# A hybrid decoder step on one core: prompt attention with float32r sums over keys, two heads in turn, and 16 page buffers

## The chip, the core and the metric

One NeuronCore of a Trainium2 chip runs the whole program. The engines work side by side, each through its own queue in order: PE (TensorE, matrix products; PEld is its loading of weights), DVE (VectorE), ACT (ScalarE), POOL (GpSimd) and SP (SyncE, which issues most DMAs here). The metric is the device time of one execution in microseconds (us), the median of three runs.

## What is computed

One inference step of a trunk of four layers. Layer 2 is the one with attention; the others mix tokens by a state space model (0, 3) or pooling (1). Each is followed by a feed-forward part (FFN) with a short convolution. There is a prompt of 272 tokens (16 learned ones and 256) and 8 decode sequences of 4 new tokens with 1024 past ones each, whose keys and values lie in 64 pages of 128 tokens in a paged cache. Attention is of the stick-breaking kind, cut to what matters:

```python
z = einsum('bqhd,bshd->bhqs', q, k) * scale + bias          # 16 heads of 64
mask = k_pos[None, :] < q_pos[:, None]
log_not = where(mask, log_sigmoid(-z), 0)
between = cumsum(log_not, axis=3, reverse=True) - log_not   # a sum over later keys
wts = where(mask, exp(log_sigmoid(z) + between), 0)
o = einsum('bhqs,bshd->bqhd', wts, v)
```

So each head needs scores, a softplus of them, a sum of it over all later keys, an exponential, and a weighted sum of values.

## The kernel before

**Precision.** The large projections split each operand in a rounded high half and the rest, both float32r, and add three products (`mm3`, L248 to L250). The attention's own products are float32: the profile shows each of them as two records of PE.

**Weights.** A plan lists all weight blocks and cache pages in order of use. Each goes by DMA from SP's queue into one of 8 places of `raw` (4 KB per partition each); for the pages of attention there are `NX` more places in `rawx`. A planner (`build_plan`) gives each load the place that it reckons to be free first. `split_blocks` makes `hi` (ACT, L208) and `lo` (DVE, L211) of a weight block, four buffers each; pages are used as they come. SP works strictly in the order of the plan, so a load whose place is not free holds back all later ones.

**The attention stage.** After the projection to q, k and v, one loop over units `u` does the decode part: `keys_t(u)` transposes a quarter of four key pages on PE (eight transposes, L1332) and copies them out as `kt` (ACT L1337, DVE L1338); two units later `keys(u)` multiplies them with the queries (four products of 256 columns, L1351, each for one range of 32 columns of the array); `scores`, `weights` and `weights_t` turn 16 units of scores into weights; `values(u)`, six slots of four units behind, multiplies two value pages with them (four products of 512 columns, L1415, in four such ranges). 64 key pages and 64 value pages of 512 KB pass through.

The prompt part is strewn in between from `u` = 22 on, one step every two units, for pairs of heads `d` = 0 to 7: `prompt_z(d)` makes scores z of two heads (L1477, 272 columns for the first 128 keys, L1478, 144 for the next 128), adds bias and mask (L1480) and takes the softplus L (DVE L1268, ACT L1269 and L1270, DVE L1271). `prompt_c(d)` sums L over later keys: a product with a triangle of ones `tri` within a block of 128 keys, one with all `ones` for the block behind it, and one for the last 16 keys (`L2`). z minus that sum (L1496), exponential (L1497). `prompt_o(d)` multiplies the weights with the values of the prompt, head after head (L1506 to L1508); the two heads of a pair write different halves of the columns of one PSUM bank. The order on each engine is set by a scheduler at build time, which starts from this program order.

`kt` has six buffers of 512 columns, two a unit; `wT`, the transposed weights of the decode part, two of 1024 columns.

Of the kernel before, what the change touches and what calls it, by code (L numbers as in the profile page):

```python
# [9 lines left out]
F32 = mybir.dt.float32  # L10
# [6 lines left out]
DM = 1024  # L17
# [23 lines left out]

LAG = 6
LEAD = 2
NX = 5


def bc(ap, pos, n):
# [13 lines left out]
class Trunk:  # L61
# [1211 lines left out]
    def attention(self, l):  # L1273
        nc, I, O = self.nc, self.I, self.O
        v = nc.vector
        with self.tc.tile_pool(name="att", bufs=1) as ap:
# [5 lines left out]
            vp2, vs = vx[64:80], vx[0:32]  # L1282
            self.rawx = ap.tile([128, NX, 1024], F32, name="rawx")
            kp = [ap.tile([128, DM], F32, name="kp", tag="z", bufs=2) for _ in range(2)]
            kp2 = ap.tile([48, DM], F32, name="kp2", tag="wT", bufs=2)

            msk = ap.tile([128, 416], F32, name="msk")
            nc.gpsimd.memset(msk, 0.0)
# [3 lines left out]
                                        fill=NEG, base=-1, channel_multiplier=-1)  # L1292
            tri = ap.tile([128, 128], F32, name="tri")
            nc.gpsimd.affine_select(out=tri, in_=self.ones, pattern=[[-1, 128]], compare_op=ALU.is_ge, fill=0.0, base=0, channel_multiplier=1)
            bB = ap.tile([128, 16], F32, name="bB")
            nc.scalar.dma_start(bB, I["attn_logit_bias"][0].partition_broadcast(128))
            self.build_dec_masks(ap, bB)
# [20 lines left out]
            def keys_t(u):  # L1318

                sl, dd = divmod(u, 4)  # L1320
                key = [self.page("k", sl, i) for i in range(4)]
                if dd == 0:
                    kt["raw"] = [self.key_page(k) for k in key]
                raw = kt["raw"]
                pts = []
                for s in range(2):
                    pt = self.bank()
                    pts.append(pt.rearrange("p (a k) -> p a k", a=2))
                    for r in range(2):
                        d = 4 * r + dd  # L1330
                        for g in range(2):
                            nc.tensor.transpose(pt[:, r * 256 + g * 128:r * 256 + (g + 1) * 128], raw[2 * s + g][:, d * 128:(d + 1) * 128], self.ident)  # L1332
                if dd == 3:
                    for k in key:
                        self.key_done(k)
                kt[u] = [ap.tile([128, 2, 256], F32, name="kt", tag="kt", bufs=6) for _ in range(2)]
                nc.scalar.activation(kt[u][0], pts[0], AF.Copy)  # L1337
                v.tensor_copy(kt[u][1], pts[1])  # L1338

# [38 lines left out]
            def weights_t(p):  # L1378

                w = zw.pop(p)  # L1380
                wT = ap.tile([128, 8, 128], F32, name="wT", tag="wT", bufs=2)
                wn = ap.tile([32, 128], F32, name="wn", tag="wn", bufs=2)
                for i in range(2):
                    pt = self.bank()
# [85 lines left out]
            def prompt_z(d):  # L1470

                PW[d] = []
                for h in range(2):
                    hs = slice(h * 64, h * 64 + 64)
                    head = 2 * d + h
                    pt = self.bank()
                    nc.tensor.matmul(pt[:, 0:NP], kT[hs, d, 0:128], qT[hs, d, 0:NP], start=True, stop=True)  # L1477
                    nc.tensor.matmul(pt[:, NP:416], kT[hs, d, 128:256], qT[hs, d, 128:NP], start=True, stop=True)  # L1478
                    z = ap.tile([128, 416], F32, name="zp", tag="zp", bufs=4)
                    v.scalar_tensor_tensor(z, pt[:, :416], bB[:, head:head + 1], msk, ALU.add, ALU.add)  # L1480
# [3 lines left out]
                    PW[d].append((z, L))  # L1484

            def prompt_c(d):
                for h in range(2):
                    head = 2 * d + h
                    z, L = PW[d][h]
# [226 lines left out]
```

## Time and profile before

| | us |
|---|---|
| median of three runs | 1666.96 |
| the three runs | 1663.04, 1667.83, 1666.96 |
| the profiled execution, device time | 1663.34 |
| its span, first to last instruction | 1661.6 |

| engine | busy us | share of the span |
|---|---|---|
| PE | 1510.3 | 91% |
| PEld | 1391.7 | 84% |
| DVE | 1206.0 | 73% |
| ACT | 829.3 | 50% |
| POOL | 546.8 | 33% |

The profile is one execution on the chip. Its page shows the time that each engine is busy, the span in 40 slices, the DMA queues, the chain of work that ended last (here 61% on PE) and the costliest groups of instructions. The trace behind it can be asked for stretches, for the instructions in order of time, and for who waited for whom. Matmuls are pipelined: records of neighbours overlap, and a product's own duration is longer than the time until the next begins.

### The profile page before, as it was taken

The page shows a single profiled execution, that of the slowest core. Times are in us where ns is not written, and L with a number is a line of the kernel's source. Part 1 is how long each engine was busy: PE and PEld are TensorE (multiplying, and loading weights), DVE is VectorE, ACT ScalarE, POOL GpSimd, SP SyncE. Part 2 cuts the span into 40 slices and gives each one's busy share as a digit, 9 for nine tenths or more (in the row PEclk, how much of TensorE's full clock was granted, in tenths as well). Part 3 has the DMA queues.
Part 4 walks back from the last instruction along what each step waited for, and adds up shares of the span by engine and source line. Part 5 has one row for each costly group of instructions (what it writes and reads, how often), then busy time and mean ns, then how long its engine had stood idle before and what let it go on. Part 6 is the DMA issues. An engine that isn't in the chain of part 4 may idle for free.

```text
span 1661.6 us, 31539 instructions
## 1 busy us (share of the span) xinstructions
PE 1510.3 (91%) x11336; PEld 1391.7 (84%) x11336; DVE 1206.0 (73%) x2513; ACT 829.3 (50%) x1483; POOL 546.8 (33%) x986
## 2 busy tenths in 40 slices
PE   3487999999899999999999988999978578999997
PEld 3376999999789999998665538999978478999997
DVE  6977589985689985644554545989877895699953
ACT  5453466654366563434444434665535333666643
POOL 7945045532265541101000000555283342144400
PEclk9978999999999999999999998999989698999999
DMA  6113455565325554564887796455524113455551
GB/s 114 15 46 120 145 153 160 153 188 164 102 90 163 161 160 150 164 216 142 300 304 273 281 372 175 148 163 158 167 83 127 32 34 94 140 168 171 156 169 47
DMA packets 220960, 256.24 MB, mean 154 GB/s; under 512 B 59045, under 2 KB 171861, under 8 KB 220720
## 3 DMA queue, kind: packets, MB, share of 16 engines
q1 hardware_dynamic: 218292, 249.15, 48.3%
q0 software_dynamic: 2368, 5.08, 0.9%
q8 instruction: 89, 1.46, 0.4%
q14 instruction: 67, 0.55, 0.1%
q10 hardware_dynamic: 144, 0.01, 0.0%
HBM read 246.78 MB, written 6.43 MB: 152 GB/s over the span
## 4 chain that ended last, share of the span: by engine, by line
PE 61%; DVE 8%; POOL 2%; issue 1%; DMA 1%; ACT 1%; SPq 0%; DVEq 0%; POOLq 0%; ACTq 0%
PE bk L248 16%; PE bk L250 16%; PE bk L249 16%; PE bk L1332 4%; PE zs L1351 2%; PE av L1415 2%; DVE lo L211 1%; DVE t L1102 1%; DVE E L1111 1%; PE bk L1491 1%; PE bk L1506 1%; DMA raw<-in_attn_w_o 1%; DVE t L1101 1%; DVE s L648 0%; PE bk L1494 0%
## 5 line engine op out<-in xcount | busy, mean ns | idle before, releaser
L208 ACT ACTIVATE hi<-raw 128x1024 fp32r<-128x1024 f32 x328 | 344.0, 1056 | 283.8 <-PE bk L249 234.7
L248 PE MATMUL bk<-uhi,hi 128*128 128x304 f32 (+1 forms) x1600 | 478.1, 303 | 7.6 <-ACT uhi L374 7.6
L249 PE MATMUL bk<-ulo,hi 128*128 128x304 f32 (+1 forms) x1600 | 482.7, 302 | 1.8 <-DVE ulo L375 1.8
L250 PE MATMUL bk<-uhi,lo 128*128 128x304 f32 (+1 forms) x1600 | 483.1, 303 | 0.0
L211 DVE TENSOR_TENSOR lo<-raw,hi 128x1024 fp32r<-128x1024 f32 x304 | 374.5, 1237 | 140.3 <-ACT hi L208 138.9
L248 PEld LDWEIGHTS bk<-uhi,hi 128*128 128x128 f32 x1600 | 300.1, 189 | 9.4 <-ACT uhi L374 8.8
L249 PEld LDWEIGHTS bk<-ulo,hi 128*128 128x128 f32 x1600 | 302.4, 189 | 3.7 <-DVE ulo L375 3.2
L250 PEld LDWEIGHTS bk<-uhi,lo 128*128 128x128 f32 x1600 | 301.8, 189 | 1.2 <-issue 0.6
L248 PE MATMUL bk<-ghi,hi 128*128 128x304 f32 (+1 forms) x704 | 212.7, 302 | 3.9 <-DVE so L531 3.2
L249 PE MATMUL bk<-glo,hi 128*128 128x304 f32 (+1 forms) x704 | 212.0, 301 | 0.0
L250 PE MATMUL bk<-ghi,lo 128*128 128x304 f32 (+1 forms) x704 | 210.8, 301 | 0.0
L467 ACT ACTIVATE c<-hx,cpT 128x320 f32<-128x320 f32 (+1 forms) x176 | 113.0, 645 | 94.0 <-DVE hx L461 92.8
L211 POOL TENSOR_TENSOR lo<-raw,hi 128x1024 fp32r<-128x1024 f32 x24 | 58.0, 2415 | 291.5 <-ACT hi L208 247.5
L459 POOL COPY hx<-stT 128x16 f32<-128x16 f32 x176 | 91.0, 522 | 159.1 <-DVE c L469 155.0
L248 PEld LDWEIGHTS bk<-ghi,hi 128*128 128x128 f32 x704 | 132.6, 188 | 5.4 <-DVE so L531 4.3
L249 PEld LDWEIGHTS bk<-glo,hi 128*128 128x128 f32 x704 | 132.7, 188 | 0.1
L250 PEld LDWEIGHTS bk<-ghi,lo 128*128 128x128 f32 x704 | 132.4, 189 | 0.0
L464 POOL COPY hp<-hx 128x2 f32<-128x2 f32 x176 | 94.6, 537 | 105.2 <-DVE hx L460 98.5
L460 DVE TENSOR_TENSOR hx<-bk,rstd 128x272 f32<-128x272 f32 (+1 forms) x176 | 76.1, 433 | 31.2 <-PE bk L250 26.1
L469 DVE SCALAR_TENSOR_TENSOR c<-hx,cpT,c 128x320 f32<-128x320 f32 (+1 forms) x176 | 94.8, 540 | 1.1
L468 DVE SCALAR_TENSOR_TENSOR c<-hx,cpT,c 128x320 f32<-128x320 f32 (+1 forms) x176 | 94.6, 540 | 0.8 <-ACT c L467 0.7
L249 PE MATMUL bk<-zlo,hi 128*128 128x304 f32 (+1 forms) x256 | 77.6, 306 | 3.6 <-DVE zlo L1167 3.6
(488 smaller groups left out, 2698.8 us busy)
## 6 DMA issues: line engine op xcount, KB each, us to landing
raw<-in_ffn_w_up SPq DMA_DIRECT2D x352, 256.0 KB
raw<-in_ffn_w_down SPq DMA_DIRECT2D x88, 512.0 KB
raw<-in_cache_v SPq DMA_DIRECT2D x46, 512.0 KB
raw<-in_cache_k SPq DMA_DIRECT2D x34, 512.0 KB
raw<-in_ssm_w_glu SPq DMA_DIRECT2D x64, 256.0 KB
rawx<-in_cache_k SPq DMA_DIRECT2D x30, 512.0 KB
raw<-in_attn_w_qkv SPq DMA_DIRECT2D x24, 512.0 KB
rawx<-in_cache_v SPq DMA_DIRECT2D x18, 512.0 KB
```

Of the source, the lines that this page charges most:

```text
L208: nc.scalar.activation(hi, raw, AF.Copy)
L211: eng.tensor_tensor(lo, raw, hi.bitcast(F32), ALU.subtract)
L248: mm(out, whi, ahi, start=start, stop=False)
L249: mm(out, whi, alo, start=False, stop=False)
L250: mm(out, wlo, ahi, start=False, stop=stop)
L459: nc.gpsimd.tensor_copy(hv[:, :, 0:2], stT[:, ft].rearrange("p (b t) -> p b t", t=2))
L460: nc.vector.tensor_tensor(h[:, 2 + t0:2 + NP], ps[:, t0:NP], self.rstd[:, t0:NP], ALU.mult)
L464: nc.gpsimd.tensor_copy(hp[:, ft], h[:, NP:NP + 2])
L467: nc.scalar.activation(o, h[:, 2 + t1:], AF.Identity, bias=par(3, ft), scale=par(2, ft))
L468: nc.vector.scalar_tensor_tensor(o, h[:, 1 + t1:HEXT - 1], par(1, ft), o, ALU.mult, ALU.add)
L469: nc.vector.scalar_tensor_tensor(o, h[:, t1:HEXT - 2], par(0, ft), o, ALU.mult, ALU.add)
L1332: nc.tensor.transpose(pt[:, r * 256 + g * 128:r * 256 + (g + 1) * 128], raw[2 * s + g][:, d * 128:(d + 1) * 128], self.ident)
```

## The change

In `prompt_z` both heads' products with 272 columns are issued first, then those with 144. The softplus L is split in two float32r halves, `lh` (a rounding copy on ACT) and `ll` (what it leaves, on DVE). In `prompt_c` the five float32 products of a head become two over all 416 columns with a float32r triangle `trr`, two of 144 columns with float32r ones `onr`, and one float32 product for the last 16 keys, which covers both places in one instruction of 2x16 columns. In `prompt_o` the heads take turns. `kt` takes the four `hi` buffers, one a unit, and `wT` the `lo` buffers of the weights, which are idle in this stage; `rawx` has 8 places instead of 5. `kp2` lies with `L`.

```diff
-NX = 5
+NX = 8
...
-            kp2 = ap.tile([48, DM], F32, name="kp2", tag="wT", bufs=2)
+            kp2 = ap.tile([48, DM], F32, name="kp2", tag="L")
...
+            trr, onr = (ap.tile([128, 128], F32R, name=n) for n in ("trr", "onr"))
+            nc.scalar.activation(trr, tri, AF.Copy)
+            nc.scalar.activation(onr, self.ones, AF.Copy)
...
-                kt[u] = [ap.tile([128, 2, 256], F32, name="kt", tag="kt", bufs=6) for _ in range(2)]
+                kt[u] = self.wp.tile([128, 1024], F32, name="kt", tag="hi", bufs=4).rearrange("p (s a k) -> p s a k", s=2, a=2)
+                kt[u] = [kt[u][:, s] for s in range(2)]
...
-                wT = ap.tile([128, 8, 128], F32, name="wT", tag="wT", bufs=2)
+                wT = self.wp.tile([128, 1024], F32, name="wT", tag="lo", bufs=4).rearrange("p (g r) -> p g r", g=8)
...
+                pts = [self.bank() for _ in range(2)]
+                for o, n, ks in ((0, NP, 0), (NP, 144, 128)):
+                    for h in range(2):
+                        hs = slice(h * 64, h * 64 + 64)
+                        nc.tensor.matmul(pts[h][:, o:o + n], kT[hs, d, ks:ks + 128], qT[hs, d, ks:NP], start=True, stop=True)
                 for h in range(2):
-                    hs = slice(h * 64, h * 64 + 64)
...
-                    nc.tensor.matmul(pt[:, 0:NP], kT[hs, d, 0:128], qT[hs, d, 0:NP], start=True, stop=True)
-                    nc.tensor.matmul(pt[:, NP:416], kT[hs, d, 128:256], qT[hs, d, 128:NP], start=True, stop=True)
...
+                    lh = ap.tile([128, 416], F32R, name="Lh", tag="Lh", bufs=2)
+                    ll = ap.tile([128, 416], F32R, name="Ll", tag="Ll", bufs=2)
+                    nc.scalar.activation(lh, L, AF.Copy)
+                    v.tensor_tensor(ll, L, lh.bitcast(F32), ALU.subtract)
+                    PW[d].append((z, lh, ll))
...
-                    nc.tensor.matmul(pc[:, 0:NP], tri, L[:, 0:NP], start=True, stop=False)
-                    nc.tensor.matmul(pc[:, 128:NP], self.ones, L[:, NP:416], start=False, stop=False)
-                    nc.tensor.matmul(pc[:, 256:NP], self.ones[64:80], L2[:, head], start=False, stop=True)
-                    nc.tensor.matmul(pc[:, NP:416], tri, L[:, NP:416], start=True, stop=False)
-                    nc.tensor.matmul(pc[:, 400:416], self.ones[64:80], L2[:, head], start=False, stop=True)
+                    nc.tensor.matmul(pc[:, 0:416], trr, lh, start=True, stop=False)
+                    nc.tensor.matmul(pc[:, 0:416], trr, ll, start=False, stop=False)
+                    nc.tensor.matmul(pc[:, 128:NP], onr, lh[:, NP:416], start=False, stop=False)
+                    nc.tensor.matmul(pc[:, 128:NP], onr, ll[:, NP:416], start=False, stop=False)
+                    nc.tensor.matmul(pc[:, 128:416].rearrange("p (a q) -> p a q", a=2)[:, :, 128:144], self.ones[64:80], bc(L2[:, head], 1, 2), start=False, stop=True)
...
-                for h in range(2):
-                    hs = slice(h * 64, h * 64 + 64)
-                    head = 2 * d + h
-                    es = slice(head * 64, head * 64 + 64)
-                    nc.tensor.matmul(po[hs, 0:NP], vp[:, 0, es], ws[h][:, 0:NP], start=True, stop=False)
-                    nc.tensor.matmul(po[hs, 128:NP], vp[:, 1, es], ws[h][:, NP:416], start=False, stop=False)
-                    nc.tensor.matmul(po[hs, 256:NP], vp2[:, es], w2[:, head], start=False, stop=True)
+                for st in range(3):
+                    for h in range(2):
...
+                        if st == 0:
+                            nc.tensor.matmul(po[hs, 0:NP], vp[:, 0, es], ws[h][:, 0:NP], start=True, stop=False)
+                        elif st == 1:
+                            nc.tensor.matmul(po[hs, 128:NP], vp[:, 1, es], ws[h][:, NP:416], start=False, stop=False)
+                        else:
+                            nc.tensor.matmul(po[hs, 256:NP], vp2[:, es], w2[:, head], start=False, stop=True)
```

The order that the scheduler makes differs on PE, ACT, DVE and SP within this stage, and in a few neighbouring rows after it. First PE at the first sums over keys (`prompt_c(0)`). The rows of before: the transposes of one unit, then one head's sums.

```order
L1332 MATMUL bk<-ident,raw 128x128 x4
L1332 MATMUL bk<-ident,rawx 128x128 x4
L1491 MATMUL bk<-Lp,tri 128x272
L1492 MATMUL bk<-Lp,ones 128x144
L1493 MATMUL bk<-L_8019,ones 128x16
L1494 MATMUL bk<-Lp,tri 128x144
L1495 MATMUL bk<-L_8019,ones 128x16
```

The same place of PE in the changed kernel (`Lh` and `Ll` are the halves `lh` and `ll`, `L_8023` is L2):

```order
L1336 MATMUL bk<-ident,raw 128x128 x8
L1502 MATMUL bk<-Lh,trr 128x416
L1503 MATMUL bk<-Ll,trr 128x416
L1504 MATMUL bk<-Lh,onr 128x144
L1505 MATMUL bk<-Ll,onr 128x144
L1506 MATMUL bk<-L_8023,ones 128x2x16
```

The first sums stay behind the same unit; each head has five products before and after, with other columns.

Next PE at the first outputs (`prompt_o(0)`), with buffer numbers, since the two heads differ by them only (zp_8929 is one head's weights, zp_8939 the other's). Before:

```order
L1415 MATMUL av_9895<-raw_70,wT_9782 32x512 x4
L1506 MATMUL bk_10048<-zp_8929,vp_7936 64x272
L1507 MATMUL bk_10048<-zp_8929,vp_7936 64x144
L1508 MATMUL bk_10048<-z2_8018,vx_7937 64x16
L1506 MATMUL bk_10048<-zp_8939,vp_7936 64x272
L1507 MATMUL bk_10048<-zp_8939,vp_7936 64x144
L1508 MATMUL bk_10048<-z2_8018,vx_7937 64x16
L1332 MATMUL bk_10057<-ident_71,rawx_7938 128x128
```

The same place in the changed kernel:

```order
L1420 MATMUL av_9910<-rawx_7938,wT_9800 32x512 x4
L1519 MATMUL bk_10069<-zp_8966,vp_7936 64x272
L1519 MATMUL bk_10069<-zp_8977,vp_7936 64x272
L1521 MATMUL bk_10069<-zp_8966,vp_7936 64x144
L1521 MATMUL bk_10069<-zp_8977,vp_7936 64x144
L1523 MATMUL bk_10069<-z2_8022,vx_7937 64x16 x2
L1336 MATMUL bk_10078<-ident_71,raw_70 128x128 x4
```

The heads now alternate product by product.

Last PE ahead of the second outputs (`prompt_o(1)`), where the four value products of one call of `values` stand together before:

```order
L1351 MATMUL zs<-kt,qb_8014 32x256 x4
L1415 MATMUL av<-raw,wT 32x512 x2
L1415 MATMUL av<-rawx,wT 32x512 x2
L1506 MATMUL bk<-zp,vp 64x272
L1507 MATMUL bk<-zp,vp 64x144
```

In the changed kernel key products stand between two and two of them:

```order
L1336 MATMUL bk<-ident,raw 128x128 x4
L1420 MATMUL av<-raw,wT 32x512 x2
L1356 MATMUL zs<-kt,qb_8018 32x256 x4
L1420 MATMUL av<-rawx,wT 32x512 x2
L1519 MATMUL bk<-zp,vp 64x272 x2
```

Over the whole stage the value products of before stand in 40 runs of at most four, those of the changed kernel in 42; the key products in 69 and 72.

## Rows read from the trace of the kernel before

**Rows 1.** Stretches: us, engines busy (instructions), clock, DMA share, GB/s.

```profile
785.00:970.00 185.00, 185.00 (x1632) 111.60 (x1630) 97.02 (x171) 82.07 (x158) 2.38 (x10) 1.00 0.82 292
970.00:991.00 21.00, 19.19 (x129) 7.14 (x129) 7.92 (x16) 5.25 (x15) 0.00 (x0) 1.00 1.02 405
```

**Rows 2.** Waits of SP's queue from 771 to 992: total us, times, longest.

```profile
SPq L186 <- PE bk L1332: 83.8, 24, 16.9
```

**Rows 3.** Timeline of PE at the end: start, us, engine, line, operation.

```profile
987.12 1.05 PE L1415 MATMUL av<-rawx,wT 128*32 128x512 f32 x4 [0.23 <-DMA rawx<-in_cache_v]
...
990.99 1.05 PE L1415 MATMUL av<-raw,wT 128*32 128x512 f32 x4 [0.26 <-DMA raw<-in_cache_v]
992.80 0.66 PE L1428 MATMUL bk<-ident,am 128*128 128x128 f32 x4 [0.76 <-ACT am L1421]
999.26 1.38 PE L248 MATMUL bk<-ohi,hi 128*128 128x304 f32 x4 [5.81 <-ACT ohi L1443]
```

**Rows 4.** Timeline of PE, sums of the first two heads.

```profile
821.08 0.62 PE L1491 MATMUL bk<-Lp,tri 128*128 128x272 f32 x2
...
821.88 0.39 PE L1493 MATMUL bk<-L,ones 16*128 16x16 f32 x2
822.20 0.51 PE L1494 MATMUL bk<-Lp,tri 128*128 128x144 f32 x2
...
824.95 0.66 PE L1332 MATMUL bk<-ident,raw 128*128 128x128 f32 x4
```

**Rows 5.** Timeline of PE, float32r products of the projections and their border.

```profile
405.71 0.28 PE L250 MATMUL bk<-shi,pwl 128*128 128x120 f32 x1
405.82 0.27 PE L248 MATMUL bk<-shi,pwh 128*128 128x120 f32 x1
...
767.25 0.30 PE L249 MATMUL bk<-ulo,hi 128*128 128x304 f32 x1
767.39 0.30 PE L250 MATMUL bk<-uhi,lo 128*128 128x304 f32 x1
767.62 0.74 PE L1477 MATMUL bk<-qT,kT 64*128 64x272 f32 x4
```

**Rows 6.** Timeline of PE, outputs of the first two heads.

```profile
835.37 0.67 PE L1506 MATMUL bk<-zp,vp 128*64 128x272 f32 x2
...
836.43 0.67 PE L1506 MATMUL bk<-zp,vp 128*64 128x272 f32 x2
...
837.49 0.33 PE L1332 MATMUL bk<-ident,rawx 128*128 128x128 f32 x1
```

**Rows 7.** Timeline of PE, decode products beside others; scores of two heads.

```profile
848.12 0.64 PE L1351 MATMUL zs<-kt,qb 128*32 128x256 f32 x8
848.57 1.04 PE L1415 MATMUL av<-raw,wT 128*32 128x512 f32 x8
849.54 0.74 PE L1477 MATMUL bk<-qT,kT 64*128 64x272 f32 x4
850.11 0.42 PE L1478 MATMUL bk<-qT,kT 64*128 64x144 f32 x4
850.46 0.33 PE L1332 MATMUL bk<-ident,rawx 128*128 128x128 f32 x1
...
875.79 1.04 PE L1415 MATMUL av<-raw,wT 128*32 128x512 f32 x2
876.76 0.66 PE L1332 MATMUL bk<-ident,rawx 128*128 128x128 f32 x4
```

**Rows 8.** Timelines of ACT, DVE and PE, from scores to sums.

```profile
854.46 0.55 ACT L1270 ACTIVATE Lp<-Lp 128x416 f32<-128x416 f32 x1
855.04 0.59 DVE L1271 TENSOR_TENSOR Lp<-Lp,zp 128x416 f32<-128x416 f32 x1 [0.32 <-ACT Lp L1270]
860.71 0.62 PE L1491 MATMUL bk<-Lp,tri 128*128 128x272 f32 x2
```

More of the change, by code (lines that the diff above doesn't have):

```diff
@@ L1472, in prompt_z @@
                 PW[d] = []
+                pts = [self.bank() for _ in range(2)]
[3 more added lines that the diff above has]
+                        nc.tensor.matmul(pts[h][:, o:o + n], kT[hs, d, ks:ks + 128], qT[hs, d, ks:NP], start=True, stop=True)
                 for h in range(2):
-                    hs = slice(h * 64, h * 64 + 64)
                     head = 2 * d + h
-                    pt = self.bank()
-                    nc.tensor.matmul(pt[:, 0:NP], kT[hs, d, 0:128], qT[hs, d, 0:NP], start=True, stop=True)
-                    nc.tensor.matmul(pt[:, NP:416], kT[hs, d, 128:256], qT[hs, d, 128:NP], start=True, stop=True)
                     z = ap.tile([128, 416], F32, name="zp", tag="zp", bufs=4)
-                    v.scalar_tensor_tensor(z, pt[:, :416], bB[:, head:head + 1], msk, ALU.add, ALU.add)
+                    v.scalar_tensor_tensor(z, pts[h][:, :416], bB[:, head:head + 1], msk, ALU.add, ALU.add)
                     L = ap.tile([128, 416], F32, name="Lp", tag="Lp", bufs=2)
@@ L1483, in prompt_z @@
                         self.softplus(L, z, v)
-                    PW[d].append((z, L))
+                    lh = ap.tile([128, 416], F32R, name="Lh", tag="Lh", bufs=2)
[3 more added lines that the diff above has]
+                    PW[d].append((z, lh, ll))
             def prompt_c(d):
@@ L1488, in prompt_c @@
                     head = 2 * d + h
-                    z, L = PW[d][h]
+                    z, lh, ll = PW[d][h]
                     pc = self.bank()
-                    nc.tensor.matmul(pc[:, 0:NP], tri, L[:, 0:NP], start=True, stop=False)
-                    nc.tensor.matmul(pc[:, 128:NP], self.ones, L[:, NP:416], start=False, stop=False)
-                    nc.tensor.matmul(pc[:, 256:NP], self.ones[64:80], L2[:, head], start=False, stop=True)
-                    nc.tensor.matmul(pc[:, NP:416], tri, L[:, NP:416], start=True, stop=False)
-                    nc.tensor.matmul(pc[:, 400:416], self.ones[64:80], L2[:, head], start=False, stop=True)
+                    nc.tensor.matmul(pc[:, 0:416], trr, lh, start=True, stop=False)
[3 more added lines that the diff above has]
+                    nc.tensor.matmul(pc[:, 128:416].rearrange("p (a q) -> p a q", a=2)[:, :, 128:144], self.ones[64:80], bc(L2[:, head], 1, 2), start=False, stop=True)
                     v.tensor_tensor(z, z, pc[:, :416], ALU.subtract)
@@ L1501, in prompt_o @@
                 po = self.bank()
-                for h in range(2):
-                    hs = slice(h * 64, h * 64 + 64)
-                    head = 2 * d + h
-                    es = slice(head * 64, head * 64 + 64)
-                    nc.tensor.matmul(po[hs, 0:NP], vp[:, 0, es], ws[h][:, 0:NP], start=True, stop=False)
-                    nc.tensor.matmul(po[hs, 128:NP], vp[:, 1, es], ws[h][:, NP:416], start=False, stop=False)
-                    nc.tensor.matmul(po[hs, 256:NP], vp2[:, es], w2[:, head], start=False, stop=True)
+                for st in range(3):
+                    for h in range(2):
+                        hs = slice(h * 64, h * 64 + 64)
+                        head = 2 * d + h
+                        es = slice(head * 64, head * 64 + 64)
+                        if st == 0:
[4 more added lines that the diff above has]
+                            nc.tensor.matmul(po[hs, 256:NP], vp2[:, es], w2[:, head], start=False, stop=True)
                 nc.scalar.activation(ohi[:, d, :NP], po[:, :NP], AF.Copy)
```

## The prediction

> **What bounds the kernel now.** I read the page of the profile first (PE busy for 91% of the span), then the busy time by stretches, to find the stage that the change touches. It runs from 772 us (transposes of the first cached key pages, next to the last products of the qkv projection) to 993 us. In its main part, 785 to 970 us, PE is busy for all of 185 us at full clock, DVE for 97 and ACT for 82 of it, and the DMA share is 0.82; in 970 to 991 us the DMA share is 1.02 [rows 1]. So PE sets the pace of the main part, and the loads set it only at the very end. A busy PE says little of what a product costs, since matmuls are pipelined; I take the time of a step from the start of its first product to the start of what follows, in the timeline of PE.
>
> The queue of loads waits 83.8 us in this stage for transposes to free a page buffer [rows 2], which fits: loads are held back by PE. At the end four pages arrive 987.12 to 990.99 us, 3.87/3 = 1.29 us apart, and the products of each wait for it [rows 3]. Then come the transposes of the last heads (992.80) and the first product of the output projection (999.26).
>
> All sums below are against the profiled execution, 1663.34 us with its span of 1661.6; it lies at the lower end of the three timed runs (1663.04 to 1667.83), whose median is 1666.96.
>
> **Sums over keys (prompt_c).** Now two heads take 824.95 - 821.08 = 3.87 us, 1.94 a head [rows 4]; there are 16. Each head gets instead two float32r products of 416 columns, two of 144, and one float32 product of 32 columns over 16 rows. No such product of 416 or 144 columns is in the trace; the nearest are the projections, also float32r: 304 columns follow each other after 0.14 us, 120 columns after 0.11 [rows 5]. By columns 416 cost 0.14 x 416/304 = 0.19, two 0.38; 144 lie between 0.11 and 0.14, I take 0.12, two 0.24. The small product cost 0.32 (821.88 to 822.20) with 16 columns [rows 4]; with 32, I keep 0.32. A change between float32r and float32 costs 0.23 - 0.14 = 0.09 (767.39 to 767.62) [rows 5]; I add 0.10 for one. A head then takes 0.38 + 0.24 + 0.32 + 0.10 = 1.04, a gain of 0.90, times 16 = **14.4 us**. Ends: 0.80 with two changes more or a dearer small product (12.8), 1.00 with no change at all (16).
>
> **Outputs (prompt_o).** Now the two heads run one behind the other, 835.37, 836.43, 837.49: 1.06 us each, 2.12 a pair, eight pairs [rows 6]. They write different halves of the columns of the array. What two products in different column ranges do is shown by the decode products: four of 256 columns, each in its own 32 columns of the array, start together and are through after 848.57 - 848.12 = 0.45 us; four of 512 columns take 0.97 (848.57 to 849.54), and a single one, cut off from its three neighbours by other work, takes the same 0.97 (875.79 to 876.76) [rows 7]. So with the heads in turn a pair costs what one head costs now, 1.06, a gain of 1.06 x 8 = **8.5 us**. Lower end 0, if halves of 64 columns don't run beside each other; the row nearest (ranges of 32) is for the gain.
>
> The Trainium skill speaks against this. "TensorE: Matmul & The Clock Gate", Part 3, "The mechanism", says that a weight load overlaps with running matmuls only when it goes to other rows of the array; both heads use all rows. By that rule the 8.5 us would not come. The decode rows contradict it so far: there too all rows are used, and four run in the time of one.
>
> **Scores (prompt_z).** The code now issues the two heads in turn as well. But in the trace of before they already run so: the four records of both 272-column products start first (849.54), then those of the 144-column ones (850.11), and all is over at 850.46, 0.92 us for two heads [rows 7], although the order before names them head by head. Gain: **0**. The skill's same section calls matmuls strictly in order, start and end; by that the heads ran in series so far, and the edit would be worth something. The rows say otherwise.
>
> **What the new order breaks.** Four decode value products belong together (above). In the order of before they stand in 40 runs where 32 would do, in the new one in 42; the key products in 69 and 72. Two more runs at 0.97 and three at about 0.55 cost 3.6 us; the last fall where PE waits for pages anyway, so **-3 us**. Ends -4 and 0.
>
> **Work added on ACT and DVE.** Per head a rounding copy on ACT (about 0.55, as the exponential of the same shape) and a subtraction on DVE (0.59) [rows 8]: 8.8 and 9.4 us in all. The cover is that both engines are busy for half of the stage: 97 + 9 of DVE in 185 - 20 us is 65%, ACT 55%. The path through them also grows. Now the scores of two heads end at 850.46, the second head's L is ready at 855.04 + 0.59 = 855.63, and the sums start at 860.71 [rows 7, 8]: 5.1 us to spare. The new steps take up to 0.55 x 2 + 0.59 of that, and the outputs in between shrink by 1.06, which leaves about 2.3 us. So 0, with an end of -3 where the scan over decode keys stands in DVE's queue at the wrong moment. Two copies of constants at the start stand behind a DMA issue on ACT's queue that has the same waits before: 0.
>
> **Key tiles, weights and page buffers.** The transposed keys go from three units in flight to four: 0 to +2. The values' weights take a buffer that the fourth block of the output projection's low half needs; it needs it after the last values either way: 0. Three more page buffers let 3 x 1.29 = 3.9 us of loads run in the idle time before 785 us. That shortens nothing where PE is the bound, and something where pages are late: 0 to +3, I take **+1**.
>
> **Do the loads keep up?** Up to 970 us the loads are busy for 0.82 x 185 = 152 us [rows 1]. With 3.9 us done earlier 148 remain, in 185 - 21 = 164 us: a share of 0.90, which they reach and pass at the end of the stage (1.02) [rows 1]. So the loads don't yet take over, though little is left.
>
> **The sum:** 14.4 + 8.5 - 3 + 1 = 21 us, all of it on PE's path in a stage that PE bounds. After the last page nothing is changed in kind: heads, splits of the output projection's blocks and its products follow as now (992.80 to 999.26 and on) [rows 3]. 1663.3 - 21 = 1642.3; with timed runs up to 3.6 us over the profiled one, I say **1643 us**.
>
> **Rivals.**
> 1. Halves of the columns don't run beside each other (the skill's rule above): the gain is 21 - 8.5 = 12.5, 1651 us. For it: the two heads of before don't overlap even at their border. Against: the decode rows. Chance 0.08.
> 2. The loads take over: PE frees pages in lumps, so the share doesn't rise beyond, say, 0.86. Then the main part takes 148/0.86 = 172 us instead of 164, 8 us are lost, 1651 us. For it: the wait for buffers, the share of 1.02 at the end. Against: three buffers more. Chance 0.10.
> 3. Slower: the way from scores to sums gets longer than the distance on PE, so that PE stands before nearly every pair's first sum. It eats the gain from 21/8 = 2.6 us of waiting a pair; with 3.5 us it costs 28 and gives about 1671 us. The distance on PE is 860.71 - 850.46 - 1.06 = 9.2 us, so the path would have to be 9.2 + 3.5 = 12.7 us; it is 5.2 now, and 1.7 come to it. Against: half-idle DVE and ACT. Chance 0.04.
> 4. It doesn't do what it says because other waits (banks, key copies) fill the place, and the time stays within 0.3%, 1662 to 1672: chance 0.04.
>
> **How the numbers follow.** My forecast has 0.74, with its own ends: 16 + 8.5 + 3 = 27.5 (1636), and 12.8 + 7 - 4 - 3 = 13 (1650). The range takes these, rivals 1 and 2 and the 3.6 us between runs: 1634 to 1654. 5 us, 0.3%, is about what a measurement can tell from no change. Faster by more: 0.74 + 0.08 + 0.10 = 0.92; the same 0.04; slower 0.04.
>
> **What would show it.** Right: a head's sums start to start in about 1.0 us, a pair's outputs in about 1.1 with both 272-column products starting together, a pair's scores still in 0.92; the last value product near 970 us, the output projection's first product some 6 us behind; PE still without gaps in the main part and the DMA share near 0.9. Wrong: outputs of 2.1 us a pair (rival 1), value or key products waiting for pages long before the end (rival 2), PE idle before a first sum with DVE's subtraction as its releaser (rival 3).

## The result and the profile after

The changed kernel takes 1640.94 us (median of four runs, 1636.96 to 1642.39) against 1666.63 (four runs, 1663.04 to 1667.83): a ratio of 0.9846, 95% interval 0.9823 to 0.9868. In a second comparison (`after_again` below) the ratio was 0.9864, 0.9843 to 0.9885. The prediction was 1643 us. Its sum of 21 us is what the stage lost (21.2), but partly by luck: two of its terms, what the three page buffers are worth and what the order breaks, were wrong, and their errors made up for 2.6 us by which the sums over keys and the outputs fell short.

The profiled execution took 1636.96 us. Busy time by stretches, as in [rows 1] (stretch, its length, PE, PEld, DVE, ACT, POOL, granted clock, DMA share, GB/s):

```profile
785.00:950.00 165.00, 164.44 (x1546) 97.51 (x1543) 106.03 (x186) 87.87 (x172) 1.87 (x8) 1.00 0.89 324
950.00:970.00 20.00, 13.31 (x95) 4.12 (x93) 6.45 (x20) 7.92 (x19) 0.00 (x0) 1.00 1.03 399
```

PE is still busy without a gap worth naming in the main part, and the DMA share has risen from 0.82 to 0.89, against 0.90 in the prediction. SP's queue waits less for transposes to free pages than in [rows 2] (total us, times, longest):

```profile
SPq L186 <- PE bk L1336: 67.0, 26, 16.9
```

A pair's outputs and two heads' sums in the timeline of PE (start, us, line, operation), which answer to [rows 6] and [rows 4]:

```profile
827.84 0.68 PE L1519 MATMUL bk<-zp,vp 128*64 128x272 f32 x4
828.35 0.42 PE L1521 MATMUL bk<-zp,vp 128*64 128x144 f32 x4
828.69 0.29 PE L1523 MATMUL bk<-z,vx 16*64 16x16 f32 x4
828.91 0.66 PE L1336 MATMUL bk<-ident,raw 128*128 128x128 f32 x4
...
832.95 0.46 PE L1502 MATMUL bk<-Lh,trr 128*128 128x416 f32 x1
833.25 0.35 PE L1503 MATMUL bk<-Ll,trr 128*128 128x416 f32 x1
833.43 0.23 PE L1504 MATMUL bk<-Lh,onr 128*128 128x144 f32 x1
833.50 0.28 PE L1505 MATMUL bk<-Ll,onr 128*128 128x144 f32 x1
833.70 0.40 PE L1506 MATMUL bk<-L,ones 16*128 16x32 f32 x2
834.04 0.46 PE L1502 MATMUL bk<-Lh,trr 128*128 128x416 f32 x1
```

A pair's outputs take 828.91 - 827.84 = 1.07 us where two heads took 2.12. A head's sums take 834.04 - 832.95 = 1.09 where they took 1.94: 0.30, 0.18, 0.07, 0.20 and 0.34 from start to start.

The end of the stage, to be read beside [rows 3]; in brackets how long PE had stood idle, and for whom:

```profile
962.21 1.05 PE L1420 MATMUL av<-raw,wT 128*32 128x512 f32 x4 [0.24 <-DMA raw<-in_cache_v]
963.49 1.05 PE L1420 MATMUL av<-rawx,wT 128*32 128x512 f32 x4 [0.23 <-DMA rawx<-in_cache_v]
965.30 0.65 PE L1433 MATMUL bk<-ident,am 128*128 128x128 f32 x4 [0.76 <-ACT am L1426]
971.76 0.62 PE L248 MATMUL bk<-ohi,hi 128*128 128x304 f32 x1 [5.81 <-ACT ohi L1448]
```

The last two pages come 1.28 us apart and PE waits for each of them; before there were four such waits. The idle 5.81 us before the output projection are the same as before.

**How the runs are compared below.** The stage is measured from the first key transposes (771.98 in the profile of before) to the first product of the output projection (999.26): 227.28 us. Within it each moment of PE goes to the product that started last, and these times are added up by kind. The table has all profiled kernels; "pieces" counts the stretches of PE in which products of that kind follow each other by their starts in the trace (the counts before the prediction and in the expectations are those of the built order, so they differ); the ratio is against the kernel before, with its interval.

| kernel | stage | sums | outputs | scores | value products (pieces) | key products (pieces) | key transposes | ratio |
|---|---|---|---|---|---|---|---|---|
| before | 227.3 | 31.7 | 17.1 | 6.8 | 46.6 (33) | 35.9 (68) | 65.3 | |
| before_again | 227.2 | 31.7 | 17.1 | 6.8 | 46.5 (33) | 35.9 (68) | 65.3 | 1.0008 (0.9991 to 1.0024) |
| after | 206.1 | 18.0 | 10.5 | 7.2 | 43.6 (37) | 37.9 (74) | 65.1 | 0.9846 (0.9823 to 0.9868) |
| after_again | 205.7 | 18.0 | 10.5 | 7.2 | 43.1 (37) | 37.9 (74) | 65.1 | 0.9864 (0.9843 to 0.9885) |
| outs_only | 221.4 | 31.7 | 10.0 | 6.8 | 47.8 (33) | 35.9 (68) | 65.3 | 0.9970 (0.9952 to 0.9988) |
| scores_only | 224.8 | 31.5 | 17.1 | 6.8 | 44.1 (33) | 36.2 (67) | 65.0 | 1.0000 (0.9983 to 1.0018) |
| mem_only | 217.1 | 31.6 | 17.0 | 6.4 | 37.7 (26) | 35.5 (66) | 65.1 | 0.9944 (0.9926 to 0.9961) |
| mem5 | 227.5 | 31.7 | 17.1 | 6.8 | 46.8 (33) | 35.9 (68) | 65.3 | 1.0000 (0.9986 to 1.0014) |
| no_outs | 215.1 | 18.0 | 18.7 | 7.2 | 42.9 (36) | 38.0 (74) | 65.1 | 0.9918 (0.9898 to 0.9939) |
| pages5 | 231.0 | 17.8 | 9.7 | 9.2 | 56.3 (61) | 46.2 (97) | 67.6 | 1.0022 (1.0004 to 1.0039) |
| small_r | 214.8 | 17.9 | 9.4 | 6.3 | 52.5 (46) | 37.2 (78) | 66.1 | 0.9921 (0.9897 to 0.9946) |
| rigid | 200.2 | 18.1 | 10.0 | 7.2 | 42.1 (27) | 34.5 (63) | 64.6 | 0.9839 (0.9817 to 0.9860) |
| rigid5 | 208.0 | 17.6 | 9.8 | 7.4 | 49.0 (34) | 35.1 (65) | 65.4 | 0.9887 (0.9866 to 0.9908) |
| before_rigid | 222.2 | 31.5 | 17.0 | 7.3 | 43.5 (28) | 34.5 (63) | 64.8 | 0.9969 (0.9957 to 0.9980) |

What is left of a stage (decode transposes, the last heads, the end of the qkv projection) is 24 to 25 us in every kernel.

### The profile page after: what moved, and what is told of

Same layout as the page of the kernel before. It is cut to its first block, busy times and chain, and to the rows that moved or that the text cites. A ratio compares the mean times of both kernels' runs of the same rounds, so it can differ in the third digit from the quotient of the medians.

```text
span 1635.3 us, 31426 instructions
## 1 busy us (share of the span) xinstructions
PE 1482.1 (91%) x11272; PEld 1372.5 (84%) x11272; DVE 1214.7 (74%) x2529; ACT 835.4 (51%) x1501; POOL 543.9 (33%) x986
## 3 DMA queue, kind: packets, MB, share of 16 engines
q8 instruction: 89, 1.46, 0.4%
## 4 chain that ended last, share of the span: by engine, by line
PE 60%; DVE 8%; POOL 2%; DMA 1%; issue 1%; ACT 1%; SPq 0%; DVEq 0%; ACTq 0%; POOLq 0%
PE bk L248 16%; PE bk L250 16%; PE bk L249 16%; PE bk L1336 4%; PE zs L1356 2%; PE av L1420 2%; DVE lo L211 1%; DVE t L1102 1%; DVE E L1111 1%; DMA raw<-in_attn_w_o 1%; DVE s L648 1%; DVE t L1101 1%; PE bk L1482 0%; DVE t L1118 0%; DVE X L1121 0%
## 5 line engine op out<-in xcount | busy, mean ns | idle before, releaser
L460 DVE TENSOR_TENSOR hx<-bk,rstd 128x272 f32<-128x272 f32 (+1 forms) x176 | 76.1, 433 | 31.5 <-PE bk L250 26.7
```

The source lines that it names most:

```text
L460: nc.vector.tensor_tensor(h[:, 2 + t0:2 + NP], ps[:, t0:NP], self.rstd[:, t0:NP], ALU.mult)
```

## Experiments

**1. How far does a profile repeat?** In the two first profiles the changed kernel is already 6.3 us ahead when the attention begins (765.71 against 771.98), in code that is the same. Both kernels ran again unchanged.

> The kernel before, unchanged, with a profile of its own. The changed kernel's profile is 6 us ahead at the attention's first transposes (765.71 against 771.98) although nothing differs up to there. Theory A, the first 500 us vary from run to run by some us: the first transposes stand anywhere between 765 and 775. Theory B, each program has its own fixed start: 772 within 1 us. The time is that of before in either case, within 2 us.

> The changed kernel, unchanged, with a profile of its own. Theory: the way to the attention varies from run to run (before_again stood at 767.58 where the first profile of the same kernel had 771.98), while the stage itself repeats: from the first key transposes to the first product of the output projection 206.1 us within 0.5, against 227.3 and 227.2 before; the time is 21 us below before on this chip, ratio 0.987. Rival: the 6 us ahead at the start belong to the changed program: the first transposes stand at 765.7 again, the ratio is 0.984.

The first key transposes of `before_again` start at 767.58, those of `after_again` at 768.91. So the lead belongs to the executions, not to the program: the rival fell. The 4.4 us between the two executions of the kernel before arise in the first 230 us; what causes them was not tried. The stage repeats to within 0.4 us (227.3 and 227.2; 206.1 and 205.7), and it is the stage that is compared from here on: 21.4 us on average. The times agree: 1639.76 against 1662.98, 23.2 us less, with 19.1 to 26.1 by the interval.

**2. Outputs alone.** The kernel before with one edit, two heads in turn:

```diff
-                for h in range(2):
+                for st in range(3):
+                    for h in range(2):
...
+                        if st == 0:
+                            nc.tensor.matmul(po[hs, 0:NP], vp[:, 0, es], ws[h][:, 0:NP], start=True, stop=False)
...
```

> The kernel before with one edit: the outputs of a pair's two heads in turn (prompt_o). My theory (halves of 64 columns run beside each other): a pair's outputs take about 1.06 us instead of 2.12, the gain is 8.5 us on PE, less what of it lies where the last pages set the pace (one or two pairs): 6 to 8.5 us, 1658 to 1661. Rival, the rule that a weight load overlaps only with products in other rows: a pair still takes 2.1 us and the time stays at 1666. The way to the attention's first transposes is the same code as before: 771.98 us if the program fixes it, otherwise some us away.

```profile
833.28 0.68 PE L1508 MATMUL bk<-zp,vp 128*64 128x272 f32 x4
833.79 0.41 PE L1510 MATMUL bk<-zp,vp 128*64 128x144 f32 x4
834.14 0.29 PE L1512 MATMUL bk<-z,vx 16*64 16x16 f32 x4
834.36 0.33 PE L1332 MATMUL bk<-ident,rawx 128*128 128x128 f32 x1
```

1.08 us a pair, and 10.0 us instead of 17.1 in all. The order of the decode products is that of before; the value products take 1.2 us longer (0.9 of it in the last 28, where PE waits for pages), and of the 7.1 us 5.9 remain. The time fell by 4.9 us (1658.06 against 1662.99), within the theory. Halves of 64 columns run beside each other although both use all rows. The rule of the Trainium skill that the prediction weighed ("TensorE: Matmul & The Clock Gate", Part 3, "The mechanism") doesn't hold here. Another page of the Trainium skill, "TensorEngine Tiling (Array Packing)", section "Key Properties", states what the rows show: different tiles of the array can load weights and multiply in parallel.

**3. Scores alone.** The edit of `prompt_z` in the kernel before.

> The kernel before with one edit: the scores of a pair's two heads issued in turn (prompt_z). My theory: they ran beside each other already, a pair takes 0.92 us as before, the time stays within 1 us of before. Rival, products strictly in order: the two heads ran in series so far, and the edit is worth up to half of 0.92 us in each of eight pairs, 3.7 us, 1663.

The pair of heads, now one group of eight records:

```profile
844.48 0.97 PE L1477 MATMUL bk<-qT,kT 64*128 64x272 f32 x8
845.38 0.33 PE L1332 MATMUL bk<-ident,rawx 128*128 128x128 f32 x1
```

0.90 us, as before (0.92), and 6.8 us of scores in both: the edit itself is worth nothing. The stage is nevertheless 2.5 us shorter, all of it in the value products (46.6 to 44.1); the time doesn't show it (ratio 1.0000, 0.9983 to 1.0018). What else differs is the order: 90 of the stage's 1868 records of PE are of another kind than at the same place in before, none of them in `outs_only` and `mem5`. That was the first sign that the order has a price of its own.

**4. The moves in memory alone**, with eight page buffers and with five. The kernel before with

```diff
-NX = 5
+NX = 8
...
-                kt[u] = [ap.tile([128, 2, 256], F32, name="kt", tag="kt", bufs=6) for _ in range(2)]
+                kt[u] = self.wp.tile([128, 1024], F32, name="kt", tag="hi", bufs=4).rearrange("p (s a k) -> p s a k", s=2, a=2)
```

and the like for `wT` and `kp2`; in `mem5` the first of these lines stays as it was.

> The kernel before with the moves in memory alone: key tiles and value weights in the weight buffers, eight extra page buffers instead of five; products as before. My theory: three pages more in flight and deeper key tiles are worth 1 to 3 us, and since the order of this kernel has the decode value products in fewer pieces than before (26 instead of 32, at about 0.5 us each) some 3 us more may come: 1661 to 1665. Rival: PE bounds the stage and waits for no page, so 0, 1666. If the 6 us by which the changed kernel was ahead when the attention began come from where things lie in memory, the first transposes stand near 766 us here, otherwise near 772.

> The kernel before with key tiles and value weights in the weight buffers, but five extra page buffers as before; PE's order in the attention is that of before, row for row. It splits mem_only's 10.2 us of the stage. Theory (the page buffers do it, by whole quadruples and fewer waits at the end): stage 227.3 within 1 us, value products 46.6 us as in before. Rival (the fourth unit of key tiles does it): stage 222 us or less.

`mem5`: 227.5 us, nothing. `mem_only`: 217.1, so the three page buffers alone are worth 10.4 us in the kernel before, where I had put 1, and the time (1652.32 us) is below what the theory and the rival for `mem_only` said. The value products have 9.1 of it: 3.6 at the very end (the last 28 products take 7.5 us instead of 11.1, with no wait for a page) and 5.5 in what came earlier. There the difference looks like this, in the timeline of before:

```profile
868.63 1.03 PE L1415 MATMUL av<-raw,wT 128*32 128x512 f32 x4
869.59 0.74 PE L1477 MATMUL bk<-qT,kT 64*128 64x272 f32 x4
870.15 0.41 PE L1478 MATMUL bk<-qT,kT 64*128 64x144 f32 x2
870.48 1.05 PE L1415 MATMUL av<-rawx,wT 128*32 128x512 f32 x4
871.47 0.51 PE L1478 MATMUL bk<-qT,kT 64*128 64x144 f32 x2
```

and in that of `mem_only`:

```profile
864.55 0.60 PE L1416 MATMUL av<-rawx,wT 128*32 128x512 f32 x2
864.56 0.60 PE L1416 MATMUL av<-raw,wT 128*32 128x512 f32 x2
864.98 0.60 PE L1416 MATMUL av<-rawx,wT 128*32 128x512 f32 x2
864.99 0.60 PE L1416 MATMUL av<-raw,wT 128*32 128x512 f32 x2
865.52 0.74 PE L1478 MATMUL bk<-qT,kT 64*128 64x272 f32 x4
```

One product is two records, so x4 are two products. Before, the two of one page run at 868.63 and take 0.96 us, the two of the other page (`rawx`) come after the scores and take 0.99. In `mem_only` all four together take 865.52 - 864.55 = 0.97. With three more buffers the scheduler leaves the quadruple whole (why it does so can't be read from a trace).

**5. The changed kernel without its parts.** `pages5` is the changed kernel with `NX = 5`, `no_outs` has the outputs head by head.

> The changed kernel with five extra page buffers instead of eight. My term of the prediction: 1 us (0 to 3) slower. The theory formed after mem_only (the moves in memory alone were worth 10.2 us of the stage, 8.9 of it in the decode value products: 3.6 us fewer waits for pages at the end and 5.3 us from quadruples kept whole): about 4 us more waiting at the end, and as much again for products in more pieces (value products in 46 pieces instead of 34, key products in 82 instead of 70): stage 212 to 217 us, 6 to 11 us slower.

> The changed kernel with the outputs head by head again. Theory: outputs cost 17.1 us of PE's path instead of 10.5, all of it on the path, stage 212.7, 6 to 7 us slower. Rival, the loads have become the bound of the changed kernel: the value products at the end wait less by as much (they wait about 2.9 us there), so 3 to 4 us slower.

`pages5` missed its theory by 14 us and is no faster than the kernel before: without the three buffers the faster products are worth nothing (227.5 for the old products in `mem5`, 231.0 for the new ones). PE is busy all the same; it runs pieces:

```profile
891.54 0.68 PE L1519 MATMUL bk<-zp,vp 128*64 128x272 f32 x4
892.05 0.41 PE L1521 MATMUL bk<-zp,vp 128*64 128x144 f32 x2
892.39 0.63 PE L1356 MATMUL zs<-kt,qb 128*32 128x256 f32 x4
892.95 0.46 PE L1521 MATMUL bk<-zp,vp 128*64 128x144 f32 x2
```

Two key products cut the pair's 144-column outputs in two, and are themselves half a quadruple: 0.56 us, the price of a whole one. At the end of this kernel a smaller part of the 25 us has another source. PE waits 2.08 us for the last decode weights (0.56 in the changed kernel), and right behind it the granted clock is at the lower of its two levels, 1.2 instead of 2.4 GHz, for some us (stretch 966 to 980: 0.76):

```profile
966.00:980.00 14.00, 11.92 (x65) 3.70 (x61) 5.63 (x7) 3.31 (x6) 0.00 (x0) 0.76 0.95 380
```

Four steps there (973.22 to 979.80) took 6.6 us; at full clock the same shapes take 0.98 + 0.99 + 0.98 + 0.59 = 3.5. `no_outs` and `small_r` have such a stretch too (0.66 from 965 to 980, and 0.54 from 963 to 974). In `no_outs`:

```profile
965.67 1.97 PE L1391 MATMUL bk<-ident,z 128*128 128x128 f32 x8 [1.46 <-ACT z L1381]
967.43 0.42 PE L1398 MATMUL bk<-ident,z 128*32 128x128 f32 x1
```

The eight transposes take 1.76 us where the changed kernel takes 0.92 (951.00 to 951.92). All steps of `no_outs` from 965.67 to 975.92 take 10.25 us, the same ones of the changed kernel 5.94 (951.00 to 956.94): 4.3 us of its stage time are the lower clock, and as much in `small_r`.

`no_outs` is 9.3 us slower in the stage than the changed kernel. The outputs cost 18.7 us instead of 10.5: seven pairs 2.12 each instead of 1.07, the last one, with the waits in and behind it, 3.83 instead of 2.94. Of the 9.3 us 4.3 are the lower clock, 1.2 of them in the last 28 value products, which wait for no page here and take 8.3 us instead of 9.3 to 9.7. At full clock the run would be 5.0 us slower if the pages were still in place, and at most 7.6 if those products then waited as in the changed kernel. The theory's 6 to 7 lies in between, the rival's 3 to 4 does not; how much of the gain the loads take, from nothing to 2.6 us, this run can't tell.

**6. No float32 product in the sums.** L2, the softplus of the last 16 keys, as two halves as well:

```diff
-                    nc.tensor.matmul(pc[:, 128:416].rearrange("p (a q) -> p a q", a=2)[:, :, 128:144], self.ones[64:80], bc(L2[:, head], 1, 2), start=False, stop=True)
+                    p2 = pc[:, 128:416].rearrange("p (a q) -> p a q", a=2)[:, :, 128:144]
+                    nc.tensor.matmul(p2, onr[64:80], bc(L2h[:, head], 1, 2), start=False, stop=False)
+                    nc.tensor.matmul(p2, onr[64:80], bc(L2l[:, head], 1, 2), start=False, stop=True)
```

> The changed kernel with one step more: the sums over the last 16 keys (L2) also as two float32r halves, so that no product of a head's sums is float32; seven extra page buffers instead of eight, to make room. In the changed kernel the float32 product and the borders beside it take 0.20 + 0.34 us of a head's 1.09. Theory: two float32r products of 32 columns take 0.1 each at most, a gain of 0.3 us a head, 5 us, stage 201 us. Rival: the loads are the bound at the end of the stage, the gain returns as waits of the last value products (they have 2.9 us already): 0 to 2 us, and one buffer fewer costs 1.

```profile
839.01 0.28 PE L1508 MATMUL bk<-Ll,onr 128*128 128x144 f32 x1
839.21 0.28 PE L1510 MATMUL bk<-L2h,onr 16*128 16x32 f32 x1
839.35 0.26 PE L1511 MATMUL bk<-L2l,onr 16*128 16x32 f32 x1
839.53 0.46 PE L1505 MATMUL bk<-Lh,trr 128*128 128x416 f32 x1
```

0.20, 0.14 and 0.18 us, as with the float32 product (0.20, then 0.34 for its two passes). Both theories missed: the sums take 17.9 us as before. It is not the change of precision that costs, but the change from 128 rows to 16 and back: of the two 144-column products of a head the first, ahead of one with 128 rows, takes 0.07 us, and the second, ahead of one with 16, takes 0.20. The kernel before shows it in float32 alone. In the sums of [rows 4] the first head's 272-column product (821.08) stands behind transposes with 128 rows, the second's (822.97) behind a product with 16:

```profile
821.54 0.41 PE L1492 MATMUL bk<-Lp,ones 128*128 128x144 f32 x2
...
822.97 0.72 PE L1491 MATMUL bk<-Lp,tri 128*128 128x272 f32 x2
823.53 0.41 PE L1492 MATMUL bk<-Lp,ones 128*128 128x144 f32 x2
```

The first takes 821.54 - 821.08 = 0.46 us, the second 823.53 - 822.97 = 0.56. Where the rows stay at 128 and only the precision changes there is no border: in `rigid5` 0.30 us pass from the start of a float32 transpose (856.98) over a float32r product of 416 columns to the next such product (857.28), 0.11 and 0.19. The Trainium skill, "TensorEngine Tiling (Array Packing)", "Key Properties", says that a change of the tiling mode, not just of the tile, drains the engine; the border of the rows agrees with it, 0.10 us for 272 columns. The rows are not the whole price: the two products with 16 rows and 32 columns follow each other only after 0.14 us, twice what 144 columns take with 128 rows; why was not tried. The value products take 9 us more than in the changed kernel (52.5, in 46 pieces), some 3 of it at the lower clock; whether the buffer that is missing or the other order of this kernel does the rest was not separated.

**7. Whole quadruples.** If pieces are the price, binding the order must give it back. A context that queues instructions behind an earlier one of PE makes key transposes, key products and value products follow each other as the code names them:

```diff
+            def after():
+                return self.tc.issue_after(seen[0].ins) if seen[0] else nullcontext()
...
-                    keys_t(u + LEAD)
+                    with after():
+                        keys_t(u + LEAD)
```

and the same around `keys(u)` and `values(c)`, where `seen[0]` is the last such product or transpose. `rigid` is the changed kernel so bound, `rigid5` the same with five buffers, `before_rigid` the kernel before.

> The changed kernel with the order of PE bound in one respect: key transposes, key products and value products of the decode part follow each other as the code names them, so that no transpose of keys gets in between the four products of a quadruple (key products then stand in 63 pieces, nearly all whole, instead of 70; value products in 27 instead of 34). Theory P (pieces): a product in a piece of its own costs what four together cost, so whole quadruples give back 2 to 3 us of key products and 3 to 5 us of value products; stage 198 to 202 us instead of 205.9, time 4 to 7 us below the changed kernel. Rival (loads): PE is held by pages; the gain comes back as waits of the last value products, 0 to 2 us.

> The same bound order with five extra page buffers instead of eight. pages5 took 231.0 us for the stage, 25 more than with eight buffers, with value products in 46 pieces and key products in 82. Theory P: those 25 us are the price of pieces, 56.3 - 35 us of value and 46.2 - 35.5 us of key products, so with whole quadruples (33 and 64 pieces) most of it is gone: stage 203 to 212 us. Rival (loads): with five buffers the loads can't keep up with the faster products; PE then stands idle for pages instead, and the stage stays at 222 us or more.

> The kernel before with the same bound order (key products in 63 pieces instead of 67, value products in 28 instead of 32), nothing else. Theory P: 3 to 6 us of the stage's 227.3 are gone, as value products are whole; what remains against the bound order with five buffers and the new products (rigid5) is then the price of the products themselves, 13.7 + 6.6 = 20 us. Rival (loads): the last value products wait by as much longer, stage 226 to 228.

All three stages fell in the ranges of theory P. The price of the products did not: `before_rigid` and `rigid5` are 14.2 us apart instead of 20. Sums and outputs are 21.1 us shorter, but 5.5 return in the value products: 2.1 in the last 28 (10.6 and 12.6 us), where pages are late, and 3.4 ahead of them, in 34 pieces instead of 28. `rigid5` takes 208.0 us: with the same five buffers and the same products as `pages5`, 23 us are gone, 11.1 of key and 7.3 of value products, 2.2 of transposes, 1.8 of scores. Some 5 of the 23 are not whole quadruples but the longer wait and the lower clock at the end of `pages5`, which `rigid5` doesn't have (it waits 0.76 us there). Key products stand whole:

```profile
887.99 0.64 PE L1361 MATMUL zs<-kt,qb 128*32 128x256 f32 x8
888.56 0.66 PE L1341 MATMUL bk<-ident,raw 128*128 128x128 f32 x4
```

four in 0.57 us. The rival, that five buffers can't feed PE, is refuted for the stage as a whole; but the loads do set the pace of the end. In `rigid5` six late pages come 1.27 to 1.32 us apart (from 966.02 to 972.46), in `rigid` four:

```profile
956.80 1.05 PE L1425 MATMUL av<-rawx,wT 128*32 128x512 f32 x4 [0.23 <-DMA rawx<-in_cache_v]
958.08 1.05 PE L1425 MATMUL av<-rawx,wT 128*32 128x512 f32 x4 [0.23 <-DMA rawx<-in_cache_v]
959.37 1.05 PE L1425 MATMUL av<-raw,wT 128*32 128x512 f32 x4 [0.24 <-DMA raw<-in_cache_v]
960.66 1.05 PE L1425 MATMUL av<-rawx,wT 128*32 128x512 f32 x4 [0.24 <-DMA rawx<-in_cache_v]
```

`rigid` has the lowest median of all, 1636.34 us, with a stage 5.4 to 5.8 us shorter than the changed kernel's (its interval overlaps that of `after_again`; the two were not timed in one comparison, and the medians are 3.4 us apart, so the time alone doesn't show the gain). The key products have 3.4 us of it, a little more than theory P says. The value products, 42.1 us, have only 1.0 to 1.5: ahead of the last 28 they are 2.3 us shorter, while the last 28 wait for pages and take 10.5 us instead of 9.3 to 9.7. That much is the rival's.

**The stage in one table** (us), which shows that products and buffers don't add up while the order is free:

| | five buffers | eight buffers |
|---|---|---|
| free order, old products | 227.5 | 217.1 |
| free order, new products | 231.0 | 205.7 to 206.1 |
| bound order, old products | 222.2 | not tried |
| bound order, new products | 208.0 | 200.2 |

With a free order the new products are worth -3.5 us with five buffers (about +1 without the wait and the lower clock at the end of `pages5`) and 11.2 with eight. With a bound order they are worth 14.2 with five.

## Why the prediction was right, and where it was not

- **The bound** was read correctly: PE is on the path through the whole stage, and its share of waits stays small. Of the stage, 21.2 us are gone in the first pair of profiles; the sum said 21.
- **Sums, 14.4 predicted, 13.7 measured** (31.7 to 18.0). A head takes 1.09 us instead of 1.04. By products: two of 416 columns 0.30 + 0.18 (I had 0.38), two of 144 0.07 + 0.20 (0.24), the small one 0.34 (0.32); the 0.10 that I had added for a border lie in the first of each group. The size is nearly right, the reason for the border was wrong (experiment 6): the row from which it was read, 767.39 to 767.62 in [rows 5], changes the rows too, from 128 to 64.
- **Outputs, 8.5 predicted, 6.6 measured.** Seven of the eight pairs take 1.07 as predicted. The last takes 2.94, where it took 2.12: its heads come apart, and PE waits for ACT's exponential between them and for the decode weights behind them (the two waits below). The prediction gave this term no such loss, and its own ends don't agree: the text has 0 as the lower one, the sum of the ends 7.
- **Scores, 0 predicted, 0 measured** (6.8 and 7.2, the rest being splits by other work).
- **What the order breaks, -3 predicted.** This step failed. It counted pieces and gave each one a full price. The price hangs on what cuts: half a quadruple that key products cut, in other columns, runs beside them, as in the changed kernel; one that scores or transposes cut costs 0.96 (experiment 4). Value products ahead of the last stretch (the last 28) take 35.5 us before and 33.9 after, in more pieces; key products 35.9 and 37.9. Together -0.4. A cut by key products, in the changed kernel, where four value and four key products take 844.13 - 842.69 = 1.44 us, as much as whole ones (0.97 + 0.45 in [rows 7]):

```profile
842.69 0.62 PE L1420 MATMUL av<-raw,wT 128*32 128x512 f32 x2
842.72 0.63 PE L1356 MATMUL zs<-kt,qb 128*32 128x256 f32 x4
843.14 0.60 PE L1420 MATMUL av<-raw,wT 128*32 128x512 f32 x2
...
844.13 0.68 PE L1519 MATMUL bk<-zp,vp 128*64 128x272 f32 x4
```

- **Page buffers, +1 predicted.** This step failed too. It saw the buffers as 3.9 us of earlier loads and as fewer late pages at the end (that part is 11.1 to 9.7, 1.4 us). Their main work is on the order that the scheduler makes. In all they are worth 10.4 us in the kernel before (3.6 of it at the very end) and 25 in the changed one (some 5 of it a longer wait and the lower clock). The two mis-sized terms met in the sum, since the pieces had been counted in the order of the finished change, with its eight buffers in it: -3 + 1 = -2 against +1.0 measured. That these 3 us made up for the 2.6 that sums and outputs fell short was luck.
- **ACT and DVE, 0 predicted**: PE waits once for ACT's exponential of the prompt (`zp`) and once for the decode weights (`z`), 0.6 us each. The kernel before has neither wait, so 1.1 us are lost here:

```profile
PE bk L1519 <- ACT zp L1508: 0.6, 1, 0.6
PE bk L1391 <- ACT z L1381: 0.6, 1, 0.6
```

- **Key tiles, 0 to +2 predicted**: 0 (`mem5`).
- **Rivals.** 1 (halves in series) fell by the 1.07 us a pair. 2 (loads) fell for the main part: the share reached 0.89 where 0.86 was its case. 3 (the path from scores to sums) fell: no wait of a first sum is in the list of PE's waits. 4 (other work fills the place) is what `pages5` became, by another cause than the prediction named: without the three buffers the change would have come out within 0.3% of the kernel before.
- The median fell by 25.7 us in the first comparison, and by 23.2 in the second, of which the stage explains 21; the rest is about what the way to the attention varied by between two executions (4.4 us in experiment 1), though no run shows that it comes from there. It was not foreseen, and no step earned it.

## What to carry to other kernels

Where a scheduler fixes the order from its own reckoning, a buffer more or a product less is also another order. Price it by building the parts and reading which groups that share the array come apart, and by what they are cut, not by counting pieces alone. Before faster products are judged, bind the order of the groups that run beside each other: here that gave back 23 us of the stage with five buffers (some 5 of them a wait and a lower clock that went with the free order) and over 5 with eight.

## What the runs showed of the hardware

- Two products in different halves of 64 columns, both with all 128 rows, run in the time of one: 1.07 us against 2.12.
- From its start to the next, a float32r product of 416 columns takes 0.18 us and one of 144 columns 0.07, inside a group of 128 rows. Ahead of a product with 16 rows the latter takes 0.13 more, and the first of the next group takes 0.30 instead of 0.18 (behind value products in their ranges of 32 columns too, 832.95 to 833.25). In float32 a product of 272 columns takes 0.56 behind a product with 16 rows and 0.46 behind transposes with 128.
- A float32 product of 32 columns over 16 rows costs what two float32r ones do: 0.34 against 0.32.
- Near the end of the stage the granted clock was at its lower level (0.50, 1.2 GHz) behind an idle time of PE of 1.46 us (`no_outs`, from 965.7 to 975.9), 1.67 (`small_r`, 963.8 to 974.1) and 2.08 (`pages5`, 972.9 to 979.7); eight 128-column transposes took 1.76 us instead of 0.92 in `no_outs`. It stayed at 1.00 (2.4 GHz) in the changed kernel behind idle times of 0.56, 0.56 and 0.86 us there, and in `pages5` behind one of 1.40 (to 987.41). What decides it was not tried.
